# Both output gates ahead of the mLSTM, two expert buffers in the tokens' place, and ranks tile by tile in a hybrid mLSTM, HGRN2 and mixture-of-experts layer

## The chip, the cores and the metric

The kernel runs on one core of one Trainium2 chip. The metric is the device time of one execution in microseconds (us). Three runs of the kernel before took 1246.77, 1248.19 and 1250.08 us; the median is 1248.19 us.

## The reference

One layer of a diffusion backbone works on 256 latent tokens of width 1024, beside 256 context tokens that only feed the scans. All is float32.

```python
h = modulate(rms_norm(x, norm1_g), sh1, sc1)      # adaLN: six vectors from silu(c) @ w_ada
p = h @ w_in                                       # one projection, split into columns
yl_ml = sigmoid(p_o)  * head_rms(bidirectional mLSTM(q, k, v, gates), norm_g)   # 4 heads of 128
yl_hg = silu(p_go)    * head_rms(bidirectional HGRN2(q, f, i), norm_g)          # 4 heads of 128
x = x + g1 * (concat([yl_ml, yl_hg]) @ w_out)
h2 = modulate(rms_norm(x, norm2_g), sh2, sc2)
logits = h2 @ router_w + router_b                  # 32 experts
top_val, top_idx = top_k(logits, 4); gates = softmax(top_val)
# for every expert e on the tokens that chose it:
gu = xe @ w_gu[e] + b_gu[e]; glu, lin = split(gu)
y_e = (min(glu, 7) * sigmoid(1.702 * glu) * (clip(lin, -7, 7) + 1)) @ w_down[e] + b_down[e]
x = x + g2 * sum over a token's experts of gate * y_e
out = rms_norm(x, final_g)
```

## The kernel before

The latent tokens are two tiles of 128 (a = 0, 1). The kernel has two halves. The first is the mixer: norm1 and adaLN (row-vector products `gemv`, L259), the input projection, the two scans, the output projection and the router. The second is a loop over the 32 experts.

*The mixer.* The weights of a projection are split into a rounded part `wh` (ScalarE, L89) and a remainder `wl` (VectorE, L90), and the tokens into `hh` and `hl`; a product is three matmuls (L314 to L316 for products by tokens). `out_gate(c0, f0, silu)` computes one group's output gate from 1024 KB of `w_in` twice, in 96 matmuls, and stores it in `og`. Before, the HGRN2's gate (`out_gate(3600, 512, True)`) stands ahead of `rows(2, 1)`, the last `gemv`; the mLSTM's (`out_gate(1024, 0, False)`) is written behind `mlstm(0)` and `mlstm(1)`, stored by a copy (L659), and made a sigmoid in one later activation (L869). Its tokens `hh`, `hl` keep their place until then.

`mlstm(tau)` makes two passes (one for each direction) for a token tile: matmuls that spread the stabiliser `NM` (L739) and the mask (L742), exponentials on ScalarE (L751), a product with the scores on VectorE (L752), matmuls with the values `mv` (L759), and the normalisation into `ym` (L763 to L771). `through` (L782 to L784) multiplies a slice of the mixer's output by a split slice of `w_out`: 48 matmuls for the HGRN2's half, 36 split and 8 plain ones (L802) for the mLSTM's. `gated(a)` normalises `ym`, multiplies by `og` (L707), transposes (L791) and splits into `yTh`, `yTl` (L776, L777).

*From the mixer to the experts.* `project(a)` finishes the output projection of a tile and makes, in halves of 512 columns, `h2 = po * g1b` (L803), `x2 = x2 + h2` (L804), `h2 = x2 * sc2` (L805), and the sum of squares (L806). `finish(a)` transposes `h2` (L813), copies it (L814), takes the inverse root (L96 to L106), multiplies by the router's weights `rw` (L819), and picks the top four: `lg` (L820), maximum, `sel`, the tie-breaking scan (L827), `sel` again (L829), and the gates (L830 to L835). `norm2(a)` completes `h2`: tile 0 on GpSimd (L842, L843), tile 1 on VectorE (L845). Then the rank of each token within its expert: matmuls of `sel` with a triangle and with ones (L913 to L915), `posm` (L916, L918), and the counts of each expert (L920 to L924), which a conditional part behind the loop reads. Only with both tiles' ranks and `h2` can `dispatch` build the selection `S` (L945) and gather an expert's tokens by matmul (L955).

*The experts.* Expert e needs 12 MB: four loads of `w_gu` and two of `w_down`, each of 2 MB (L128). They go through buffers of 2 MB in pools that `slot()` takes in turn from the list `rings`. There are nine at the end: `ring` (3, from the start), `ring2` (3, in the mLSTM's and tokens' place on the right side, after `right_m.close()`), `ring3` (2, after `mixed.close()`) and `ring4` (1, after `front.close()`). All loads are issued in one order by the SyncE queue; a load waits for its buffer, and the ones behind it wait too. The products are L973 (`pu`), transposes L983 (`pt`), the activation, L1007 (`pd`), and the sum over experts L1019.

The order of instructions on each engine is chosen when the kernel is built: the framework's scheduler puts work in by priority and dependency, and `tc.issue_after` adds an ordering by hand. Engines then run their own list in order.

Of the kernel before, what the change touches and what calls it, by code (L numbers as in the profile page):

```python
# [28 lines left out]
def tile_hybrid_backbone(  # L29
# [26 lines left out]
    ones = fc.tile([128, 128], FT)  # L56
# [91 lines left out]
    shc = fo.tile([128, 8], FT, name="shc")  # L148
    dr = ctx.enter_context(tc.tile_pool(name="dr", bufs=1, space=bass.MemoryType.DRAM))
# [4 lines left out]
    right_m = ExitStack()  # L154
    fm = right_m.enter_context(tc.tile_pool(name="fm", bufs=1, side="right"))
    yh = fm.tile([128, 2, 512], FT, name="yh")
    mk = fm.tile([128, 2, 512], FT, name="mk")
    mq = fm.tile([128, 2, 256], FT, name="mq")
    bcol = fm.tile([128, 9, R], FT, name="bcol")
    NM = fm.tile([R, 256], FT, name="NM")  # L160
    mv = fm.tile([128, 4, 4, 130], FT, name="mv")
# [982 lines left out]
```

## Time and profile before

| | |
|---|---|
| median of three runs | 1248.19 us |
| profiled execution | 1248.19 us |
| its span (first to last instruction) | 1246.4 us |
| TensorE busy | 1136.3 us, 91% |
| VectorE busy | 423.2 us, 34% |
| ScalarE busy | 250.0 us, 20% |
| moved by the DMA queue of the weights | 452.08 MB, 87.1% of the 16 DMA engines' span |

An engine's busy share is over the whole span; stages have different limits. Time is read best in stretches: the window view gives for each stretch the busy time of every engine, the TensorE clock that was granted (1.00 is 2.4 GHz, 0.50 is 1.2 GHz), the share of DMA time in use and the rate in GB/s. The timeline gives single instructions with their start, and in brackets how long their engine had stood idle before and what released it.

### The profile page before, as it was taken

The page shows a single profiled execution, that of the slowest core. Times are in us where ns is not written, and L with a number is a line of the kernel's source. Part 1 is how long each engine was busy: PE and PEld are TensorE (multiplying, and loading weights), DVE is VectorE, ACT ScalarE, POOL GpSimd, SP SyncE. Part 2 cuts the span into 40 slices and gives each one's busy share as a digit, 9 for nine tenths or more (in the row PEclk, how much of TensorE's full clock was granted, in tenths as well). Part 3 has the DMA queues.
Part 4 walks back from the last instruction along what each step waited for, and adds up shares of the span by engine and source line. Part 5 has one row for each costly group of instructions (what it writes and reads, how often), then busy time and mean ns, then how long its engine had stood idle before and what let it go on. Part 6 is the DMA issues. An engine that isn't in the chain of part 4 may idle for free.

```text
span 1246.4 us, 14117 instructions
## 1 busy us (share of the span) xinstructions
PE 1136.3 (91%) x5790; PEld 566.7 (45%) x5791; DVE 423.2 (34%) x935; ACT 250.0 (20%) x469; POOL 102.3 (8%) x199
## 2 busy tenths in 40 slices
PE   4899999998999999989999987998899789879985
PEld 1688887886534343443334322532253234324321
DVE  5478968676112221312121211121211121112124
ACT  3577455562110000001000100100010001000001
POOL 4000002002110110120001100200020002000001
PEclk9899999997999999999999999999999999999998
DMA  9723556639799999999999999999999999999993
GB/s 372 240 73 131 202 199 235 241 124 428 326 429 426 427 427 426 415 427 427 426 427 427 428 426 429 426 427 428 427 426 426 428 428 427 427 426 427 428 427 158
DMA packets 52068, 457.30 MB, mean 367 GB/s; under 512 B 4375, under 2 KB 20848, under 8 KB 24480
## 3 DMA queue, kind: packets, MB, share of 16 engines
q1 hardware_dynamic: 50096, 452.08, 87.1%
q0 software_dynamic: 1584, 3.74, 0.9%
q8 instruction: 47, 0.77, 0.3%
q10 hardware_dynamic: 320, 0.53, 0.1%
q14 instruction: 21, 0.17, 0.0%
HBM read 455.27 MB, written 1.06 MB: 366 GB/s over the span
## 4 chain that ended last, share of the span: by engine, by line
PE 57%; DMA 37%; DVE 3%; ACT 1%; issue 1%; SPq 0%; POOL 0%; DVEq 0%; ACTq 0%
DMA w<-w_down_dram 21%; PE pu L973 19%; DMA w<-w_gu_dram 15%; PE pd L1007 7%; PE pm L955 4%; PE pm L1019 4%; PE pj L299 3%; PE pj L298 2%; PE pj L300 2%; DMA w<-w_ada_dram 2%; PE pj L259 2%; PE pt L983 1%; PE pj L316 1%; PE pj L314 1%; PE pj L315 1%; PE m L759 1%
## 5 line engine op out<-in xcount | busy, mean ns | idle before, releaser
L973 PE MATMUL pu<-w,XT 128*64 128x512 f32 x2048 | 456.4, 595 | 33.6 <-DMA w<-w_gu_dram 33.5
L973 PEld LDWEIGHTS pu<-w,XT 128*64 128x64 f32 x2048 | 142.7, 137 | 324.7 <-issue 270.3
L1007 PE MATMUL pd<-w,aT 128*64 128x512 f32 x1024 | 231.4, 597 | 17.6 <-DMA w<-w_down_dram 15.7
L1007 PEld LDWEIGHTS pd<-w,aT 128*64 128x64 f32 x1024 | 70.0, 137 | 153.8 <-issue 126.6
L990 DVE TENSOR_TENSOR gl<-pt,bgT 128x512 f32<-128x512 f32 x32 | 22.1, 692 | 335.4 <-PE pt L983 335.3
L76 ACT ACTIVATE gu<-pu 128x512 f32<-128x512 f32 x48 | 26.9, 595 | 490.9 <-PE pu L973 477.5
L78 DVE COPY gu<-pu 128x512 f32<-128x512 f32 x16 | 11.1, 692 | 244.0 <-ACT gu L76 244.0
L945 POOL TENSOR_SCALAR S<-islot,posm 128x64 f32<-128x64 f32 x60 | 25.9, 454 | 662.0 <-PE pm L955 473.1
L1010 DVE TENSOR_TENSOR YP<-pd,g2b 64x512 f32<-64x512 f32 x64 | 44.0, 688 | 93.7 <-PE pd L1007 92.9
L955 PEld LDWEIGHTS pm<-S,h 128*128 128x128 f32 x512 | 65.1, 201 | 17.4 <-issue 16.0
L955 PE MATMUL pm<-S,h 128*128 128x128 f32 x512 | 68.7, 290 | 2.2 <-DVE S L945 1.0
L1019 PE MATMUL pm<-YP,GT 128*128 128x512 f32 x128 | 61.1, 611 | 8.0 <-DVE YP L1010 8.0
L298 PE MATMUL pj<-hh,wh 128*128 128x512 f32 (+1 forms) x160 | 57.7, 368 | 3.1 <-ACT hh L361 3.1
L299 PE MATMUL pj<-hl,wh 128*128 128x512 f32 (+1 forms) x160 | 59.0, 369 | 0.1
L300 PE MATMUL pj<-hh,wl 128*128 128x512 f32 (+1 forms) x160 | 57.3, 362 | 0.0
L90 DVE TENSOR_TENSOR wl<-w,wh 128x1024 fp32r<-128x1024 f32 x39 | 47.5, 1222 | 28.0 <-ACT wh L89 27.8
L957 ACT ACTIVATE XT<-pm 128x512 f32<-128x512 f32 x32 | 19.0, 597 | 176.9 <-PE pm L955 176.9
L983 PEld LDWEIGHTS pt<-ident,gu 128*128 128x128 f32 x256 | 33.7, 210 | 35.6 <-ACT gu L76 19.7
L993 ACT ACTIVATE sg<-gl 128x512 f32<-128x512 f32 x32 | 20.2, 630 | 143.1 <-DVE gl L991 143.1
L983 PE MATMUL pt<-ident,gu 128*128 128x128 f32 x256 | 40.3, 298 | 9.1 <-ACT gu L76 9.1
L89 ACT ACTIVATE wh<-w 128x1024 fp32r<-128x1024 f32 x39 | 41.0, 1060 | 26.6 <-PE pj L299 20.1
L1019 PEld LDWEIGHTS pm<-YP,GT 128*128 128x128 f32 x128 | 22.4, 189 | 46.9 <-issue 30.0
(457 smaller groups left out, 1148.8 us busy)
## 6 DMA issues: line engine op xcount, KB each, us to landing
w<-w_gu_dram SPq DMA_DIRECT2D x128, 2048.0 KB, 34.8
w<-w_down_dram SPq DMA_DIRECT2D x63, 2048.0 KB, 35.9
w<-w_ada_dram SPq DMA_DIRECT2D x12, 2048.0 KB, 8.9
w<-w_in_dram SPq DMA_DIRECT2D x16, 1024.0 KB, 8.9
w<-w_out_dram SPq DMA_DIRECT2D x2, 2048.0 KB, 8.2
w<-w_down_dram SPq DMA_DIRECT2D x4, 512.0 KB, 30.1
xin<-x_dram SPq DMA_DIRECT2D x2, 512.0 KB, 4.1
xin<-ctx_dram SPq DMA_DIRECT2D x2, 512.0 KB, 5.7
```

What stands on the lines that cost most here:

```text
L76: act(o, i, AF.Copy)
L89: act(wh, src, AF.Copy)
L90: dve.tensor_sub(wl, src, wh.bitcast(FT))
L298: mm(o, wh[:, s], hh[:, k, t0:], start=(k == 0), stop=False)
L299: mm(o, wh[:, s], hl[:, k, t0:], start=False, stop=False)
L300: last_p[0] = mm(o, wl[:, s], hh[:, k, t0:], start=False, stop=(k == 7))
L955: mm(p_[:, i * ns:(i + 1) * ns], hv[:, a, (k + i) // 2, i % 2], S[:, a, 0:nj].rearrange("p j s -> p (j s)"), start=(a == 0), stop=(a == 1))
L973: mm(ps[64 * j:64 * j + 64, n * 512:(n + 1) * 512], XT(k), w[:, k % 2, j * 1024 + n * 512:j * 1024 + (n + 1) * 512], start=(k == 0), stop= ...
L983: nc.tensor.transpose(pt[:, f * 128:(f + 1) * 128], sv[:, f // 4, f % 4], ident)
L1007: mm(pd_[64 * n:64 * n + 64, :], aT[:, k], w[:, i, n * 512:(n + 1) * 512], start=(k == 0), stop=(k == 7))
L1010: dve.tensor_mul(yp[:, f], pd_[64 * n:64 * n + 64, :], g2b[64 * n:64 * n + 64, f])
L1019: mm(p_, GTs[j][0:ns, a * 128:(a + 1) * 128], YP[0:ns, j, n * 512:(n + 1) * 512], start=(j == 0), stop=(j == np_ - 1))
```

## The change

- The mLSTM's output gate moves up, behind `rows(2, 1)` and ahead of the mLSTM. Both gates are stored by a sigmoid directly; the copy, the later sigmoid and an exponential that only loaded a table go. The mLSTM's exponentials are ordered behind the last sigmoid.
- The tokens' place (`right`) is closed right there, and a pool `ring2` of two expert buffers opens in it. Both halves of `w_out` are loaded ahead of the mLSTM.
- The mLSTM's place becomes three fixed tiles (`place(0)` to `place(2)`), which later hold `x2`, `g2b` and `h2`. The other pools are `ring3` (1), `ring4` (2) and `ring5` (1): nine buffers as before, taken by the expert loop in a new order.
- The scale `sc2` is moved into the router's weights (`rws = rw * scc`, with `scc` from four more transposes in `rows(2, 1)`), so the router takes transposes of `x2` and not of `h2`.
- The sum of squares of a tile is added up in `project`; `h2 = x2 * sc2` comes behind it; `project(1)`'s VectorE and ScalarE work is ordered behind tile 0's sum (`late`).
- `rank(a)` makes the ranks of a tile, tile 0's from `sel` of tile 0 alone; `gates(a)` is a step of its own; `counts()` moves into the expert loop, at e = 5.

```diff
@@ out_gate @@
-            if silu:
-                act(o, ps, AF.Sigmoid)
+            last_s[0] = act(o, ps, AF.Sigmoid)
+            if silu:
                 dve.tensor_mul(o, o, ps)
-            else:
-                act(o, ps, AF.Copy)
...
@@ project, finish, rank @@
+        if late[0] is not None:
+            st_.enter_context(tc.issue_after(late[0].ins))
...
             dve.tensor_mul(h2[:, a, f], po_[a][n], g1b[:, f])
             dve.tensor_add(x2[:, a, f], x2[:, a, f], h2[:, a, f])
+            act(po_[a][n], x2[:, a, f], AF.Square, accum_out=ss[:, 2 * n + a:2 * n + a + 1])
+        late[0] = dve.tensor_add(ss[:, a:a + 1], ss[:, a:a + 1], ss[:, 2 + a:3 + a])
+        for n in range(2):
             dve.tensor_mul(h2[:, a, f], x2[:, a, f], sc2[:, f])
...
-                nc.tensor.transpose(p_[:, i * 128:(i + 1) * 128], h2[:, a, (k + i) * 128:(k + i + 1) * 128], ident)
+                nc.tensor.transpose(p_[:, i * 128:(i + 1) * 128], x2[:, a, (k + i) * 128:(k + i + 1) * 128], ident)
...
-            mm(pl[:, 0:NE], hT2[:, a, k], rw[:, k], start=(k == 0), stop=(k == 7))
+            mm(pl[:, 0:NE], hT2[:, a, k], rws[:, k], start=(k == 0), stop=(k == 7))
...
+    def rank(a, p_):
+        mm(p_[:, a * NE:(a + 1) * NE], tri, sel[:, a], start=(a == 0), stop=True, skip_group_check=True)
+        if a == 0:
+            mm(p_[:, NE:2 * NE], ones, sel[:, 0], start=False, stop=False, skip_group_check=True)
+        dve.scalar_tensor_tensor(posm[:, a], p_[:, a * NE:(a + 1) * NE], 1.0, sel[:, a], op0=OP.add, op1=OP.mult)
+        dve.tensor_scalar(posm[:, a], posm[:, a], -1.0, None, op0=OP.add)
@@ the main program @@
     out_gate(3600, 512, True)
     rows(2, 1)
+    out_gate(1024, 0, False)
+    right.close()
+    ring2 = ctx.enter_context(tc.tile_pool(name="ring2", bufs=NR2, side="right", reuse_waits="tile"))
+    wh_ = load_blocks(w_out[0], 512, 4, 0)
+    wm_ = load_blocks(w_out[0], 0, 4, 0)
...
     mlstm(0)
     mlstm(1)
-    out_gate(1024, 0, False)
...
     project(0)
     finish(0)
+    rk = bank()
+    rank(0, rk)
+    gates(0)
     project(1)
...
     finish(1)
+    rank(1, rk)
     norm2(1)
+    gates(1)
...
+    rings[:] = [(ring2, NR2), (ring, NR), (ring3, NR3), (ring4, NR4), (ring5, NR5)]
+    loaded[0] = 0
```

The built programs show what moves. Lines of the changed kernel have other numbers: L320 to L322 are the gate's matmuls, L743 and L746 the spreading of `NM` and of the mask, L764 the matmuls with the values, L787 to L789 `through`, L812 the plain half of `project`, L827 the router's transposes, L832 its product, L846 and L848 the ranks, L965 the dispatch.

TensorE from the last `gemv` into the mLSTM, before (`pj<-ident,yh` are the transposes of the HGRN2's output, L314 to L316 the mLSTM's gate):

```order
L259 MATMUL pj<-w,silr 32x512 x16
L855 MATMUL pj<-ident,yh 128x128 x4
L739 MATMUL m<-NM,ident 128x128 x3
L855 MATMUL pj<-ident,yh 128x128 x4
L739 MATMUL m<-NM,ident 128x128
L739 MATMUL t<-NM,ident 128x128 x4
L742 LDWEIGHTS idb
L742 MATMUL t<-mneg,idb 128x512
L314 MATMUL pj<-wh,hh 128x256
L315 MATMUL pj<-wl,hh 128x256
L316 MATMUL pj<-wh,hl 128x256
```

and in the changed kernel, from the end of the same gate (`fm_108` holds `yh`, `fm_109` holds `NM`):

```order
L321 MATMUL pj<-wl,hh 128x256
L322 MATMUL pj<-wh,hl 128x256
L883 MATMUL pj<-ident,fm_108 128x128 x8
L743 MATMUL m<-fm_109,ident 128x128 x4
L743 MATMUL t<-fm_109,ident 128x128 x4
L746 LDWEIGHTS idb
L746 MATMUL t<-mneg,idb 128x512
L787 MATMUL pj<-wh,yTh 128x512
L788 MATMUL pj<-wl,yTh 128x512
L787 MATMUL pj<-wh,yTh 128x512
L788 MATMUL pj<-wl,yTh 128x512
```

All 96 gate matmuls now stand ahead of the transposes and of the mLSTM, and the matmuls of `through` stand between its steps where the gate's stood.

TensorE from the end of the output projection to the dispatch, before (`h_2713` is `h2`; L906 transposes the expert biases):

```order
L906 MATMUL t<-ident,bgs 128x128 x4
L813 MATMUL m<-ident,h_2713 128x128 x8
L819 MATMUL m<-rw,hT_1927 128x32 x4
L813 MATMUL m<-ident,h_2713 128x128 x4
L819 MATMUL m<-rw,hT_1927 128x32 x4
L813 MATMUL m<-ident,h_2713 128x128 x4
L819 MATMUL m<-rw,hT_1927 128x32 x8
L913 MATMUL m<-sel,tri 128x32
L914 MATMUL m<-sel,ones 128x32
L920 MATMUL t<-sel,ones 128x32
L915 MATMUL m<-sel,tri 128x32
L921 MATMUL t<-sel,ones 128x32
```

and in the changed kernel (`fm_2347` is `x2`; the first row is the biases):

```order
L927 MATMUL t<-ident,bgs 128x128 x4
L827 MATMUL m<-ident,fm_2347 128x128 x8
L832 MATMUL m<-rws,hT_1925 128x32 x8
L846 MATMUL m<-sel,tri 128x32
L848 MATMUL m<-sel,ones 128x32
L827 MATMUL m<-ident,fm_2347 128x128 x8
L832 MATMUL m<-rws,hT_1925 128x32 x8
L846 MATMUL m<-sel,tri 128x32
L965 MATMUL pm<-S,fm_2617 128x128 x16
```

The two tiles are no longer interleaved: tile 0 is transposed and routed first, and its ranks (L846, L848), which need `sel` of tile 0, stand ahead of tile 1's transposes. The counts are gone from here.

The SyncE queue from the load of the mLSTM's gate, before (`w_3031`, `w_3041`, `w_3051`, `w_3061` are the first expert's `w_gu` in order, `w_3095` and up the loads after them; which buffer each has follows from the pools):

```order
L135 DMA w_2484<-w_in_dram 128x8x256 x2
L119 DMA w_2620<-w_out_dram 128x4x1024
L119 DMA w_2686<-w_out_dram 128x4x1024
L128 DMA w_3031<-w_gu_dram 128x4096
L128 DMA w_3061<-w_gu_dram 128x4096
L128 DMA w_3095<-w_gu_dram 128x4096
L128 DMA w_3105<-w_gu_dram 128x4096
L128 DMA w_3041<-w_gu_dram 128x4096
L128 DMA w_3136<-w_down_dram 128x4096
L128 DMA w_3051<-w_gu_dram 128x4096
L128 DMA w_3115<-w_gu_dram 128x4096
L128 DMA w_3125<-w_gu_dram 128x4096
```

and in the changed kernel (`w_3029` to `w_3059` are the first expert's `w_gu`):

```order
L136 DMA w_2152<-w_in_dram 128x8x256 x2
L120 DMA w_2275<-w_out_dram 128x4x1024
L120 DMA w_2277<-w_out_dram 128x4x1024
L129 DMA w_3049<-w_gu_dram 128x4096
L129 DMA w_3029<-w_gu_dram 128x4096
L129 DMA w_3039<-w_gu_dram 128x4096
L129 DMA w_3059<-w_gu_dram 128x4096
L129 DMA w_3103<-w_gu_dram 128x4096
L129 DMA w_3134<-w_down_dram 128x4096
L129 DMA w_3093<-w_gu_dram 128x4096
L129 DMA w_3113<-w_gu_dram 128x4096
L129 DMA w_3123<-w_gu_dram 128x4096
```

Both have `w_out` twice and then nine loads for the experts, each in the order in which the buffers come free; `w_in` and `w_out` are now issued with nothing of the mLSTM between them.

## Rows read from the trace of the kernel before

**Rows 1.** The page: the chain that ended last, by engine.

```profile
PE 57%; DMA 37%; DVE 3%; ACT 1%; issue 1%; SPq 0%; POOL 0%; DVEq 0%; ACTq 0%
```

**Rows 2.** Windows: stretch, length, busy time (instructions) of each engine, clock, DMA share, GB/s.

```profile
800.00:1200.00 400.00, 359.77 (x1668) 137.85 (x1666) 80.94 (x135) 29.42 (x53) 19.58 (x40) 1.00 1.01 427
```

**Rows 3.** Timeline of SyncE's queue: start, duration, line, transfer, count.

```profile
239.85 34.04 SPq L128 DMA_DIRECT2D w<-w_gu_dram  x5
289.89 0.33 SPq L128 DMA_DIRECT2D w<-w_down_dram  x1
291.61 5.94 SPq L128 DMA_DIRECT2D w<-w_gu_dram  x3
320.25 0.34 SPq L128 DMA_DIRECT2D w<-w_down_dram  x1
```

**Rows 4.** Timeline of TensorE, from the output projection's end to the first expert.

```profile
295.37 1.97 PE L813 MATMUL m<-ident,h 128*128 128x128 f32 x8 [3.32 <-DVE h L805]
...
302.30 3.46 PE L819 MATMUL m<-rw,hT 128*128 128x32 f32 x16
306.04 0.64 PE L913 MATMUL m<-sel,tri 128*128 128x32 f32 x2 [0.28 <-DVE sel L829]
...
310.51 5.90 PE L955 MATMUL pm<-S,h 128*128 128x128 f32 x32 [0.96 <-DVE S L945]
...
316.55 8.80 PE L973 MATMUL pu<-w,XT 128*64 128x512 f32 x40
```

**Rows 5.** Windows: the mixer's end, the stretch behind it, and two parts of that.

```profile
230.00:291.60 61.60, 61.60 (x402) 53.39 (x401) 40.54 (x126) 36.96 (x99) 2.96 (x5) 1.00 0.63 258
291.60:316.60 25.00, 19.48 (x98) 18.45 (x97) 16.72 (x70) 7.20 (x17) 8.56 (x9) 0.59 0.92 392
294.00:298.00 4.00, 2.63 (x12) 2.34 (x12) 4.00 (x18) 2.80 (x8) 0.00 (x0) 0.53 1.02 434
314.00:318.00 4.00, 4.00 (x28) 2.98 (x28) 0.00 (x0) 1.47 (x3) 1.49 (x4) 0.91 0.13 53
```

**Rows 6.** Timeline of TensorE: matmuls of the gate, then of `through`.

```profile
243.84 0.28 PE L315 MATMUL pj<-wl,hh 128*128 128x256 f32 x1
243.96 0.28 PE L316 MATMUL pj<-wh,hl 128*128 128x256 f32 x1
...
265.81 0.39 PE L784 MATMUL pj<-wh,yTl 128*128 128x512 f32 x1
266.04 0.39 PE L782 MATMUL pj<-wh,yTh 128*128 128x512 f32 x1
```

**Rows 7.** Timeline of ScalarE: an exponential of the mLSTM, a split of its output.

```profile
261.94 0.63 ACT L751 ACTIVATE E__2450<-t,bcol 128x128 f32<-128x128 f32 x2 [1.66 <-PE t L742]
...
285.56 0.37 ACT L776 ACTIVATE yTh<-t,cols 128x128 fp32r<-128x128 f32 x1 [0.42 <-DVE yTl L777]
```

**Rows 8.** Timeline of VectorE: the mLSTM, then the router.

```profile
262.60 0.43 DVE L752 TENSOR_TENSOR E__2450<-E__2450,msT 128x256 f32<-128x256 f32 x1
...
292.22 2.49 DVE L804 TENSOR_TENSOR x<-x,h 128x512 f32<-128x512 f32 x4
...
301.64 0.25 DVE L820 SCALAR_TENSOR_TENSOR lg<-m,r,rb 128x32 f32<-128x32 f32 x1 [0.80 <-PE m L819]
...
302.62 1.61 DVE L845 SCALAR_TENSOR_TENSOR h<-h,r,sh 128x512 f32<-128x512 f32 x1
304.15 1.28 DVE L827 TENSOR_TENSOR_SCAN ce<-eq 128x32 f32<-128x32 f32 x1
...
306.68 0.24 DVE L820 SCALAR_TENSOR_TENSOR lg<-m,r,rb 128x32 f32<-128x32 f32 x1
...
307.65 0.21 DVE L827 TENSOR_TENSOR_SCAN ce<-eq 128x32 f32<-128x32 f32 x1
...
308.24 0.19 DVE L829 TENSOR_TENSOR sel<-sel,eq 128x32 f32<-128x32 f32 x1
```

**Rows 9.** Timeline of GpSimd: the second half of `norm2(0)`.

```profile
302.41 2.94 POOL L843 TENSOR_TENSOR h<-h,sh 128x512 f32<-128x512 f32 x2
```

More of the change, by code (lines that the diff above doesn't have):

```diff
@@ L55, in tile_hybrid_backbone @@
     dve.tensor_scalar(ident, jp, 0.0, None, op0=OP.is_equal)
-    ones = fc.tile([128, 128], FT)
+    ones = consts.tile([128, 128], FT)
     dve.memset(ones, 1.0)
@@ L136, in load_in @@
         return v[:, 0], v[:, 1]
-    sel = fc.tile([128, 2, NE], FT, name="sel")
+    sel = keep.tile([128, 2, NE], FT, name="sel")
     pj = front.enter_context(tc.tile_pool(name="pj", bufs=4, space=PSUM))
@@ L153, in tile_hybrid_backbone, with place @@
     R = 36
[L154 to L161, printed above, removed]
+    fm = ctx.enter_context(tc.tile_pool(name="fm", bufs=1, side="right"))
+    def place(i):
+        return fm.tile([128, (2048, 1092, 2080)[i]], FT, name=f"fm{i}")
+    p0, p1, p2 = [place(i) for i in range(3)]
+    yh, mk = [p0[:, 1024 * i:1024 * i + 1024].rearrange("p (a t) -> p a t", a=2) for i in range(2)]
+    mq = p1[:, 0:512].rearrange("p (a t) -> p a t", a=2)
+    bcol = p1[:, 512:512 + 9 * R].rearrange("p (i r) -> p i r", i=9)
+    NM = p1[0:R, 836:1092]
+    mv = p2.rearrange("p (a h d) -> p a h d", a=4, h=4)
     right = ExitStack()
@@ L865, in tile_hybrid_backbone @@
     dve.tensor_add(rb, p_[:, 0:NE], rb)
-    right.close()
-    with tc.issue_after(last_e[1].ins):
-        sg_ = act(og[:, :, 0:512], og[:, :, 0:512], AF.Sigmoid)
-    with tc.issue_after(sg_.ins):
-        act(ss[:, 0:1], one_c, AF.Exp)
     po_ = [[pj.tile([128, 512], FT, name="pj") for _ in range(2)] for _ in range(2)]
-    w = load_blocks(w_out[0], 512, 4, 0)
     for k in range(4):
-        wh, wl = halves(w[:, k])
+        wh, wl = halves(wh_[:, k])
         for a in range(2):
@@ L878, in tile_hybrid_backbone @@
                 through(a, k, wh, wl, n, k == 0)
-    w = load_blocks(w_out[0], 0, 4, 0)
-    wo = [halves(w[:, 0]), halves(w[:, 1]), halves(w[:, 2]), w[:, 3]]
+    wo = [halves(wm_[:, 0]), halves(wm_[:, 1]), halves(wm_[:, 2]), wm_[:, 3]]
     fs.close()
@@ L899, in tile_hybrid_backbone @@
     finish(0)
+    rk = bank()
+    rank(0, rk)
+    gates(0)
     project(1)
     mixed.close()
-    rings.append((ctx.enter_context(tc.tile_pool(name="ring3", bufs=NR3, side="right", reuse_waits="tile")), NR3))
+    ring4 = ctx.enter_context(tc.tile_pool(name="ring4", bufs=NR4, side="right", reuse_waits="tile"))
     norm2(0)
@@ L1022, in combine, with counts @@
                 dve.tensor_add(x2[:, a, f], x2[:, a, f], p_)
+    def counts():
+        q_ = ebank()
+        mm(q_[:, 0:NE], ones, sel[:, 0], start=True, stop=False)
+        mm(q_[:, 0:NE], ones, sel[:, 1], start=False, stop=True)
+        mx = e1.tile([1, 1], FT, name="mx")
+        dve.tensor_copy(cnt_i[:, 0:NE], q_[0:1, 0:NE])
+        dve.tensor_reduce(mx, q_[0:1, 0:NE], axis=AX.X, op=OP.max)
+        dve.tensor_copy(cnt_i[:, NE:NE + 1], mx)
     def biases():
@@ L1062, in tile_hybrid_backbone @@
             next(jobs[e - 1])
+            if e == 5:
+                counts()
             if e == 7:
```

55 lines of the change are left out of this document (23 added, 32 removed).

## The prediction

> **What bounds the kernel now.** I read the chain first: 57% of the span is TensorE, 37% DMA [rows 1], so neither VectorE nor ScalarE can be worth much except where TensorE waits for them. The windows then say which stage has which limit. In the expert loop the DMA engines are full: 427 GB/s at a share of 1.01 from 800 to 1200 us [rows 2]. A load of 2 MB (2.097 million bytes) takes 2.097/0.427 = 4.91 us there. Of 192 loads for the experts nine are issued early, by 297.5 us, because there are nine buffers: 5, 1 and 3 [rows 3]. The tenth waits at 320.25 until the first expert's product, begun at 316.55 [rows 4], has freed a buffer 3.7 us later. After it 182 loads of 4.91 us, 894 us, follow nearly without a hole, and their end sets the end of the kernel. So the time follows one event, the start of the first expert's product: what moves it by 1 us moves the end by 1 us, and what moves nothing there is worth nothing.
>
> That start comes out of two stretches. In the mixer's end, 230 to 291.6 us, TensorE is busy 61.60 of 61.60 us at a granted clock of 1.00 [rows 5]: only its own work and its waits count there. From 291.6 (call this E, the end of the output projection) to 316.55, 24.95 us pass on dependencies: TensorE idles 3.32 us before the router's first transposes at 295.37, `sel` of tile 1 ends at 308.24 + 0.19 = 308.43 [rows 8], dispatch starts at 310.51 and the product 6.04 us later [rows 4]. The clock is 0.53 in the part from 294 to 298, right behind that idle time, and 0.91 only from 314 [rows 5].
>
> The sum below goes against the profiled execution, 1248.19 us with a span of 1246.4; it equals the median of the three runs.
>
> **The mixer's end: E + 1.5 us.** No matmul goes or comes in this stretch. The sigmoid stored directly takes away a copy, a sigmoid and two table loads of ScalarE. That is worth nothing: TensorE did not wait there. What does change is the cover. A pass of the mLSTM spreads `NM`, then waits for exponentials (0.63 us a pair, [rows 7]) and a product on VectorE (0.43 us, [rows 8]) before its first matmul with the values: a chain of 1.06 us, four times. Before, the gate's 96 matmuls filled these waits; they start 0.12 us apart [rows 6], 11.5 us in all. In the new order they stand in one piece ahead of the mLSTM, and the 48 matmuls of `through` fill in, 0.23 us apart [rows 6], 11.0 us. In quantity the cover is the same. But these 48 were the cover of something else: 36 of them ran while `ym` of tile 1 was normalised, transposed and split. Now `gated` has only the 36 of the mLSTM's half behind it, and the transposes of each tile stand directly ahead of the matmuls that need the split halves. A split takes 0.37 us on ScalarE after its idle 0.42 [rows 7]; I charge 0.6 us to each tile, 1.2. For the passes I charge half a chain to the first (its `through` waits for the split of the weights) and to the last, 0.4 + 0.5 = 0.9; the two between have `through` matmuls ahead in the order. Against that, the gate in one piece spares changes between kinds of work, 0.6. Sum 1.2 + 0.9 - 0.6 = +1.5. The bounds: with no wait at all and twice that sparing, -1.2; with all four chains bare (4 x 1.06 = 4.2) and 0.8 for each tile, +5.2. The four added transposes fall in `rows(2, 1)`, ahead of this stretch, at about 0.25 us each by the eight of 1.97 us [rows 4]; most of that lies beside the gate's matmuls, and it is inside these bounds.
>
> **From E to the first expert: between -0.45 and +1.0 us, taken as +0.3.** In step with the new order on TensorE:
>
> 1. Tile 0's `x2` is ready while `project(1)` still runs, since the four additions (2.49 us together, [rows 8]) no longer stand in one row behind both tiles. So the 3.32 us of idle time goes. Behind the biases the transposes of tile 0 run from about E + 0.5, and the router's product of 16 records follows. At the 0.216 us of a record in the trace (3.46/16, [rows 4]) or half of that, `lg` of tile 0 comes at about E + 5.4; before it came at 301.64, E + 10.0.
> 2. From `lg` to `sel` took 306.68 to 308.43 = 1.75 us for tile 1, with nothing between [rows 8]. For tile 0 the two halves of `norm2(1)` stand between, at least 0.75 us each (half of the 1.61 of [rows 8] rounded down): `sel` of tile 0 at E + 8.7. Before, it released the ranks at 306.04, E + 14.4 [rows 4].
> 3. Here the 5.7 us gained are given back. TensorE works in order, and the ranks of tile 0 stand ahead of tile 1's transposes, so it idles from about E + 6 until E + 8.7. Then: ranks, two pairs by 0.64 less overlap, 0.9; eight transposes, 1.9; 16 records, 3.5; `lg` to `sel`, 1.75. `sel` of tile 1 at E + 16.8. Before: 308.43 - 291.6 = E + 16.8. The interleaved order of before had tile 1's transposes and product done while VectorE still worked on tile 0.
> 4. From `sel` to the dispatch took 2.08 us, of it 0.45 for the three operations of the counts ahead of `S`; without them 1.63. Then 6.04 as before, at the same half clock. First product at E + 24.5 instead of 24.95: -0.45.
>
> The upper value is contention of VectorE and GpSimd. Beside `norm2(0)` on GpSimd (2.94 us for the second pair, 1.47 each, [rows 9]) the scan took 1.28 us, and 0.21 when GpSimd was still [rows 8]. In the new order `norm2(0)` starts at about E + 5.3 and its second pair at E + 8.4, just when `sel` of tile 0 is due. One operation put behind one half costs 1.47: -0.45 + 1.47 = +1.0. The value taken, +0.3, is the middle. As outer bounds I keep +2.1 (the scan stretched by 1.07 too) and -2.2 (tile 1's product at full clock, 3.46/2 less).
>
> The Trainium skill (SBUF — State Buffer, "Who interferes with whom") says that a VectorE instruction with two inputs in SBUF and a GpSimd instruction that reads SBUF exclude each other for a whole instruction, and that the order of issue decides who waits. The 1.28 against 0.21 us agrees. By that rule alone the wait would be full and the sum 1248.19 + 1.5 + 1.0 = 1250.7 us.
>
> **Buffers, loads, counts: 0.** Nine loads are ahead as before. Five of them go out during the mLSTM (two into the tokens' place), the other four from E on, so the DMA engines finish earlier than before and then idle some 10 us until the first buffer is freed, where they idled some 5 (53 GB/s from 314 to 318, [rows 5]). All nine are in time either way. The `gemv`'s and `w_out`'s loads stand ahead in the queue in either kernel, so nothing waits behind a new stranger. The counts' matmuls at e = 5 lie in the DMA-bound loop. If that cover were gone, they would cost about 1 us.
>
> Sum: 1248.19 + 1.5 + 0.3 = **1250.0 us**. A measurement of this kernel can tell about 0.3%, 3.7 us, from no change: 1244.4 to 1251.9.
>
> **Rivals.**
>
> *The cover was needed (slower).* If the matmuls of `through` can't start when the passes need them, since their split weights come from the same ScalarE and VectorE that make the exponentials, every pass shows its chain and each tile its split: E + 5.2, and with +0.3 the time is 1253.7 us. It decides from E + 3.4 on, two bare chains more than I charge. For it: ScalarE is busy 36.96 and VectorE 40.54 of the 61.6 us [rows 5], so they are no idle helpers. Against: 11.0 us of cover for 4.2 us of chains.
>
> *The clock holds (faster).* TensorE is fed from E on without the 3.32 us of idle time. If it stays at 1.00, the dispatch takes half of its 5.90 us, tile 1's product half of 3.46 and its transposes half of 1.97: 5.7 us less. 1248.19 + 1.5 - 0.45 - 5.7 = 1243.5 us. Against: step 3 leaves TensorE idle at E + 6 for some 2.7 us, and the trace's clock was down right behind 3.3 idle us; it came back only in the dense work of the dispatch and the product. The Trainium skill (TensorE: Matmul & The Clock Gate, Part 1) says that the clock follows how busy the engine has been of late; the rows agree, and this rival turns on whether the new idle time is as harmful as the old.
>
> *Earlier loads shorten the stream (faster).* If the DMA hole before 320.25 (from about 315, 5.3 us) closed, the time would be 1242.9. Against: the cap is nine buffers, and the tenth load needs the first product.
>
> *The ranks are not tile by tile in effect.* Step 3 is already this case: tile 0's ranks wait at the head of TensorE's queue. If `sel` of tile 0 is late by both stretches, this is the +2.1 above, 1251.8.
>
> **How the numbers follow.** Forecast 0.52, its own range 1247 to 1252.3; uncovered mLSTM 0.29; clock 0.13; earlier loads 0.04; the remaining 0.02 lies beyond. Faster by over 0.3% comes from the two faster rivals, 0.17. Slower by over 0.3% comes from the 0.29 and a sliver of the forecast, 0.31. Between: 0.52. The range goes from 1243.5 to 1255.0: it takes in the clock's case and the slower rival with 1.3 us on top, and leaves out little more than the earlier loads.
>
> **What would show it.** The last plain matmul of `project` at 293 (right) or beyond 295 (uncovered). TensorE's idle time ahead of the first rank near 2.7 us, released by VectorE's `sel`; `sel` of tile 0 at E + 8.7 and of tile 1 at E + 16.8. The granted clock in the dispatch near 0.5; near 1.00 it would be the clock rival. The tenth load 3.7 us behind the first product, and the rate in the loop at 427 GB/s: another rate would make the whole account wrong.

## The result and the profile after

The changed kernel takes 1255.4 us (median of four runs, 1254.52 to 1256.58) where the kernel before takes 1249.13 beside it: ratio 1.0054 [1.0042, 1.0066], slower by 6.3 us. The forecast was 1250.0 us with a range of 1243.5 to 1255.0. The profiled execution took 1254.78 us, its span is 1252.9.

First the chain by engine on the page, the answer to [rows 1]:

```profile
PE 56%; DMA 35%; issue 3%; DVE 3%; ACT 1%; POOL 0%; SPq 0%; DVEq 0%; ACTq 0%; POOLq 0%
```

TensorE and DMA give up three points, and "issue" gains two. Where the time lies shows in the windows (columns as in [rows 5]): the mixer's end, the stretch from there to the first expert's product, three pieces of the first pass of the mLSTM, and the loop.

```profile
229.25:295.88 66.63, 64.89 (x406) 55.77 (x407) 43.14 (x133) 33.35 (x98) 2.97 (x5) 0.97 0.67 263
295.88:323.85 27.97, 16.12 (x93) 15.10 (x92) 16.55 (x68) 6.41 (x15) 8.37 (x9) 0.63 0.69 293
249.00:251.00 2.00, 2.00 (x13) 1.88 (x13) 1.78 (x5) 2.00 (x10) 0.00 (x0) 0.78 0.94 395
251.00:253.00 2.00, 2.00 (x10) 1.85 (x9) 0.82 (x5) 1.45 (x7) 0.00 (x0) 0.50 1.08 455
253.00:255.00 2.00, 2.00 (x13) 1.78 (x12) 1.12 (x7) 0.75 (x3) 0.00 (x0) 0.87 0.98 412
800.00:1200.00 400.00, 360.74 (x1684) 138.64 (x1683) 79.01 (x132) 30.30 (x55) 23.52 (x48) 1.00 1.01 427
```

The loop stands as in [rows 2], 427 GB/s at a share of 1.01. The mixer's end, counted from the last `gemv` to the last matmul of `project`, is 66.63 us long at a granted clock of 0.97 with 1.74 us in which TensorE is idle; before it was 61.76 us (229.82 to 291.58) and busy throughout. It begins 0.57 us earlier, so E moves from 291.58 to 295.88: **+4.30**. The stretch behind E is 27.97 us instead of 24.97: **+3.00**. Together +7.30 at the first product.

SyncE's queue, against [rows 3], shows that this goes on to the end:

```profile
234.70 48.08 SPq L129 DMA_DIRECT2D w<-w_gu_dram  x5
294.24 0.33 SPq L129 DMA_DIRECT2D w<-w_down_dram  x1
295.91 5.18 SPq L129 DMA_DIRECT2D w<-w_gu_dram  x3
327.54 0.33 SPq L129 DMA_DIRECT2D w<-w_down_dram  x1
```

The tenth load is issued at 327.54, 3.69 us behind the product at 323.85, and 7.29 us later than before. The last group of `pd` products begins 6.60 us later (1228.68 against 1222.08), the span is 6.5 us longer: the loop gives back 0.8 at most. Nine loads are still early, and the stretch behind E shows a DMA share of 0.69 where [rows 5] had 0.92: idle DMA time that costs nothing, since the tenth load waits for the first product either way.

The waits of TensorE in the mixer's end (who waits, for whom, sum, count, longest); before, this list is empty:

```profile
PE pj L787 <- ACT yTh L781: 0.9, 2, 0.5
PE t L796 <- DVE rb L897: 0.3, 1, 0.3
PE m L764 <- DVE E__2571 L757: 0.2, 1, 0.2
PE m L764 <- DVE E__2360 L757: 0.2, 1, 0.2
```

The tail on TensorE, against [rows 4]:

```profile
296.19 1.04 PE L827 MATMUL m<-ident,fm 128*128 128x128 f32 x8
297.98 1.97 PE L832 MATMUL m<-rws,hT 128*128 128x32 f32 x16 [0.75 <-ACT hT L828]
308.49 0.61 PE L846 MATMUL m<-sel,tri 128*128 128x32 f32 x2 [8.54 <-DVE sel L842]
...
309.34 1.95 PE L827 MATMUL m<-ident,fm 128*128 128x128 f32 x8
311.18 3.62 PE L832 MATMUL m<-rws,hT 128*128 128x32 f32 x16
316.66 0.64 PE L846 MATMUL m<-sel,tri 128*128 128x32 f32 x2 [1.86 <-DVE sel L842]
318.00 5.70 PE L965 MATMUL pm<-S,fm 128*128 128x128 f32 x32 [0.70 <-DVE posm L850]
...
323.85 6.66 PE L983 MATMUL pu<-w,XT 128*64 128x512 f32 x30
```

TensorE idles 8.54 us before tile 0's first rank. On VectorE, against [rows 8]:

```profile
293.19 1.29 DVE L813 TENSOR_TENSOR fm<-pj,row 128x512 f32<-128x512 f32 x2 [1.58 <-DMA row<-scr]
...
302.27 0.25 DVE L833 SCALAR_TENSOR_TENSOR lg<-m,r,rb 128x32 f32<-128x32 f32 x1
...
304.57 1.38 DVE L868 SCALAR_TENSOR_TENSOR fm<-fm,r,sh 128x512 f32<-128x512 f32 x2
...
306.05 1.07 DVE L841 SCALAR_TENSOR_TENSOR eq<-ce,cg,eq 128x32 f32<-128x32 f32 x1
307.16 1.19 DVE L842 TENSOR_TENSOR sel<-sel,eq 128x32 f32<-128x32 f32 x1
...
316.13 0.25 DVE L841 SCALAR_TENSOR_TENSOR eq<-ce,cg,eq 128x32 f32<-128x32 f32 x1
316.42 0.19 DVE L842 TENSOR_TENSOR sel<-sel,eq 128x32 f32<-128x32 f32 x1
```

and GpSimd, against [rows 9]:

```profile
302.33 3.12 POOL L865 TENSOR_SCALAR fm<-fm,r 128x512 f32<-128x512 f32 x2 [18.91 <-DVE rt L103]
305.42 2.87 POOL L866 TENSOR_TENSOR fm<-fm,sh 128x512 f32<-128x512 f32 x2
```

VectorE works without a wait of note from 293.19 to 309.1. TensorE has tile 0's product at 299.95 (297.98 + 1.97), E + 4.1, but `lg` comes at 302.27, E + 6.4, behind VectorE's other work; from there to `sel` (308.35) 6.1 us pass, since two halves of `norm2(1)` stand between (1.38 us) and most small operations beside GpSimd's 5.99 us are longer than for tile 1, when GpSimd is still: the pair ahead of `sel` takes 1.07 and 1.19 us against 0.25 and 0.19. Then the same clock as before: tile 1's product takes 3.62 us, the dispatch 5.70.

### The profile page after: what moved, and what is told of

It reads as the page before. It is cut to its first block, busy times and chain, and to the rows that moved or that the text cites. A ratio compares the mean times of both kernels' runs of the same rounds, so it can differ in the third digit from the quotient of the medians.

```text
span 1252.9 us, 14137 instructions
## 1 busy us (share of the span) xinstructions
PE 1138.8 (91%) x5794; PEld 567.0 (45%) x5795; DVE 425.6 (34%) x939; ACT 245.6 (20%) x465; POOL 102.0 (8%) x199
## 4 chain that ended last, share of the span: by engine, by line
PE 56%; DMA 35%; issue 3%; DVE 3%; ACT 1%; POOL 0%; SPq 0%; DVEq 0%; ACTq 0%; POOLq 0%
PE pu L983 19%; DMA w<-w_down_dram 18%; DMA w<-w_gu_dram 15%; PE pd L1017 10%; PE pm L965 5%; PE pm L1029 3%; PE pj L305 3%; PE pj L306 2%; PE pj L304 2%; PE pj L265 2%; PE pt L993 2%; PE pj L322 1%; PE pj L320 1%; PE pj L321 1%; PE m L547 1%
## 5 line engine op out<-in xcount | busy, mean ns | idle before, releaser
L1020 DVE TENSOR_TENSOR YP<-pd,fm 64x512 f32<-64x512 f32 x64 | 44.0, 688 | 132.6 <-PE pd L1017 131.8
L965 PEld LDWEIGHTS pm<-S,fm 128*128 128x128 f32 x512 | 66.2, 205 | 17.7 <-issue 16.3
L965 PE MATMUL pm<-S,fm 128*128 128x128 f32 x512 | 70.5, 294 | 1.9 <-POOL S L955 0.9
```

Source lines behind the costliest of these rows:

```text
L965: mm(p_[:, i * ns:(i + 1) * ns], hv[:, a, (k + i) // 2, i % 2], S[:, a, 0:nj].rearrange("p j s -> p (j s)"), start=(a == 0), stop=(a == 1))
L1020: dve.tensor_mul(yp[:, f], pd_[64 * n:64 * n + 64, :], g2b[64 * n:64 * n + 64, f])
```

## The experiments

Each was timed beside the kernel before, whose median was 1248.73 to 1249.03 us there; ratios are against it. "E" and "product" are from each one's profiled execution; "mixer" runs from the last `gemv` to E, "stretch" from E to the first expert's product.

| kernel | mixer, clock | E | stretch | product | median us | ratio |
|---|---|---|---|---|---|---|
| before | 61.76, 1.00 | 291.58 | 24.97 | 316.55 | 1249.13 | |
| after | 66.63, 0.97 | 295.88 | 27.97 | 323.85 | 1255.4 | 1.0054 [1.0042, 1.0066] |
| gate only | 66.15, 0.97 | 295.81 | 24.22 | 320.03 | 1251.55 | 1.0019 [1.0010, 1.0029] |
| gate half | 67.26, 0.97 | 297.13 | 24.26 | 321.39 | 1255.1 | 1.0055 [1.0038, 1.0071] |
| gate double | 74.38, 1.00 | 304.19 | 24.20 | 328.39 | 1260.62 | 1.0101 [1.0083, 1.0118] |
| router part only | 69.08, 0.95 | 297.32 | 30.48 | 327.80 | 1259.46 | 1.0089 [1.0072, 1.0106] |
| router part, mixer kept | 63.78, 1.00 | 293.31 | 31.31 | 324.62 | 1257.56 | 1.0071 [1.0054, 1.0088] |
| ranks late | 64.97, 1.00 | 295.96 | 22.71 | 318.67 | 1249.55 | 1.0008 [0.9999, 1.0018] |
| no GpSimd | 66.59, 0.97 | 295.80 | 26.82 | 322.62 | 1254.19 | 1.0044 [1.0030, 1.0058] |
| ranks late, no GpSimd | 68.21, 0.95 | 296.67 | 18.92 | 315.59 | 1247.05 | 0.9984 [0.9973, 0.9996] |
| ranks late, rows first | 68.18, 0.95 | 297.80 | 21.38 | 319.18 | 1248.91 | 0.9997 [0.9987, 1.0007] |
| the last two together | 66.64, 0.97 | 296.24 | 18.12 | 314.36 | 1245.6 | 0.9974 [0.9964, 0.9983] |
| mixer of before, new router | 63.78, 1.00 | 293.13 | 20.51 | 313.64 | 1245.69 | 0.9973 [0.9964, 0.9983] |

**The mixer: gate only.** The kernel before, with the mLSTM's gate ahead of the mLSTM, its sigmoid stored directly and the exponentials ordered behind it; router and buffers as before.

```diff
     rows(2, 1)
+    out_gate(1024, 0, False)
...
     mlstm(1)
-    out_gate(1024, 0, False)
```

> The kernel before with one part of the change: the mLSTM's output gate ahead of the mLSTM, stored by a sigmoid directly. Pools, loads, router and ranks stay as before. Theory A (the mixer's end got longer because the gate no longer fills the mLSTM's waits): the output projection ends 3 to 5 us later than in the kernel before, the stretch from there to the first expert stays at 25.0 us, and the time is 1252 to 1254 us. Rival B (the mixer's end got longer through the new places, the buffers or the transposes in the last rows, and the gate is innocent): the output projection ends within 1 us of before, 1249 us.

E comes at 295.81 against 295.88 of the whole change, the mixer takes 66.15 us, and the waits are the same four. So nearly all of the change's loss in the mixer comes with the gate's move alone (4.39 of 4.87 us), as A has it. The profiled product is 3.5 us later than before; by the ratio the time is up 2.4 us [1.2, 3.6], and the median lies 0.45 below A's range: the stretch behind E came out at 24.22 and not 25.0.

**Gate double.** The gate computed twice: ahead of the mLSTM, and again where it was. That adds 96 matmuls and restores the filler.

```diff
     rows(2, 1)
+    out_gate(1024, 0, False)
```

> The kernel before with the mLSTM's gate computed twice: 96 matmuls added ahead of the mLSTM (their result is overwritten), and the gate behind it in the code as before, so that its 96 matmuls still stand between the mLSTM's steps. The 96 added cost 96 x 0.12 = 11.5 us of TensorE's time if nothing else changes. Theory A (what the moved gate costs is the cover it takes from the mLSTM): with the cover back the output projection ends 11 to 12.5 us later than in the kernel before, at 302.5 to 304, and the time is 1260 to 1262 us; so the 96 matmuls between the steps cost only some 7 us of end time, since the kernel with the gate in front alone ended at 295.8. Rival B (a gate in front delays the mixer by itself, through its weights' loads or the exponentials that start later): it ends at 306 to 308, 15 us or more later, time 1264 to 1266.

The window of its mixer's end:

```profile
229.80:304.19 74.39, 74.31 (x500) 65.21 (x499) 46.57 (x133) 41.44 (x105) 2.96 (x5) 1.00 0.62 241
```

TensorE is busy for 74.31 of 74.39 us at 1.00. Against before, 96 matmuls ahead cost 74.38 - 61.76 = 12.6 us; against gate only, the same 96 as filler cost 74.38 - 66.15 = 8.2 us. The difference, 4.4 us, is by arithmetic the same as gate only less before (66.15 - 61.76); what this run adds is that a gate ahead, with the old filler kept, has neither the waits nor the drop of the clock. So both go with the filler's absence and not with the gate's early place. The time is A's, and E is 0.2 us beyond A's range. This kernel has 96 matmuls more than gate only, though: whether the amount of filler decides, or what the filler waits for, it does not tell.

**Gate half.** 48 of the 96 matmuls ahead, 48 behind.

```diff
+    out_gate(1024, 0, False, (0,))
...
-    out_gate(1024, 0, False)
+    out_gate(1024, 0, False, (1,))
```

> The kernel before with one half of the mLSTM's gate (48 of 96 matmuls) ahead of the mLSTM and the other half behind it in the code as before; storing by a copy and the later sigmoid as before. Theory A (what the gate costs in front is the cover that the mLSTM's waits lose): with half of the cover left the output projection ends at 291.5 to 293 us, TensorE idles under 1 us in the mixer's end, and the time is 1248.5 to 1250 us. Rival B (any matmuls of through inside the mLSTM cost the clock and the time): it ends at 294 to 296, time 1251 to 1252.5.

It came out later than gate only by 1.3 us at E, beyond A and B, with a wait that was not foreseen:

```profile
PE t L795 <- DVE rb L870: 2.8, 1, 2.8
```

Here the late sigmoid is kept, and ScalarE's two table loads and the activation (272.99 to 276.7) stand ahead of the splits of `w_out`; VectorE's remainders `wl` wait for these, and `rb` stands behind them. This kernel says nothing of the filler's size.

**The router part only.** The kernel before with the new `project`, `finish`, `rank`, `gates` and `counts` and the four added transposes, but its own gate and buffers.

```diff
     project(0)
     finish(0)
+    rk = bank()
+    rank(0, rk)
+    gates(0)
     project(1)
...
     finish(1)
+    rank(1, rk)
     norm2(1)
+    gates(1)
```

> The kernel before with the other part of the change: router on transposes of x2, sums and ranks tile by tile, counts in the expert loop; the gate stays behind the mLSTM, pools and loads as before. Theory A (tile 0's ranks at the head of TensorE's queue give back what tile 0 gains; the rows' late arrival and GpSimd make it worse only where the mLSTM ends late): the output projection ends within 0.5 us of before, the stretch from there to the first expert takes 22 to 25 us, time 1246 to 1249 us. Rival B (the new order of the router is itself the loss, whatever the mixer does): the stretch takes 27 to 28 us as in the changed kernel, time 1251.5 to 1253.

Neither theory held, because the mixer did not stay as it was: TensorE's order there changed with the four transposes in `rows(2, 1)`, and the mixer took 69.08 us with these waits, which are not those of the changed kernel:

```profile
PE pj L785 <- DVE yTl L778: 2.6, 1, 2.6
...
PE pj L783 <- ACT yTh L777: 1.0, 1, 1.0
```

So the transposes were put behind the mLSTM:

```diff
-            o, j = (shc, 2) if gp == 1 else (scc, 0)
-            dve.tensor_copy(o.rearrange(...), columns(bank(True), t)[:, j:j + 2, :, 0])
...
+    dve.tensor_copy(scc.rearrange(...), columns(bank(True), ars[2])[:, 0:2, :, 0])
     dve.tensor_tensor(rws, rw, ...)
```

> The router's part of the change once more on the kernel before, with its four added transposes behind the mLSTM and not in the last rows, so that the mixer's matmuls stand in nearly the order of before. Theory A (the late end of the mixer in the first run of this part came from a reshuffled order of the mixer, not from the router): the output projection ends within 1.5 us of before (291.6), the stretch behind it takes 27 to 30 us as TensorE waits for tile 0's selection, time 1252 to 1255 us. Rival B (the ordering of project(1) behind tile 0's sum holds up the mixer itself): the output projection ends at 295 to 297 us and the time is 1257 to 1260.

The mixer is at 63.78 us, 2.0 us longer than before with one wait of 1.0 for `yTh`, and the clock at 1.00. E is 1.7 us later than before and so just outside A's 1.5; the stretch is 31.31, 6.3 us longer than before and beyond A, with two long waits:

```profile
296.65 2.01 PE L828 MATMUL m<-rws,hT 128*128 128x32 f32 x16 [2.00 <-ACT hT L824]
309.44 0.60 PE L842 MATMUL m<-sel,tri 128*128 128x32 f32 x2 [10.78 <-DVE sel L838]
```

10.78 us before the first rank, and 2.0 for a copy on ScalarE behind the copy of the biases. The router part by itself is a loss, product +8.07. With gate only's +3.48 that makes 11.55, not 7.30: the parts can't be added.

Most of the difference is an order on ScalarE that the changed kernel does not have. Here the copy of the biases, which needs transposes that TensorE makes behind `project`, stands ahead of tile 0's squares; tile 0's sum needs the squares, and tile 1's additions are ordered behind that sum:

```profile
293.82 1.09 ACT L931 ACTIVATE bgT<-t 128x512 f32<-128x512 f32 x1 [5.38 <-PE t L930]
294.70 0.70 ACT L811 ACTIVATE pj<-x 128x512 f32<-128x512 f32 x1
...
296.15 0.16 DVE L812 TENSOR_TENSOR ss<-ss 128x1 f32<-128x1 f32 x1 [5.72 <-ACT pj L811]
```

VectorE idles 5.72 us, and `lg` of tile 0 comes at 302.94, E + 9.6. In the changed kernel the squares (295.11) stand ahead of the copy (296.39), `lg` comes at E + 6.4, and the stretch is 3.3 us shorter.

**Ranks late.** The changed kernel with tile 0's ranks behind tile 1's router.

```diff
     finish(0)
-    rk = bank()
-    rank(0, rk)
...
     finish(1)
+    rk = bank()
+    rank(0, rk)
     rank(1, rk)
```

> The changed kernel with the ranks of tile 0 put behind the router of tile 1, so that tile 1's transposes and product on TensorE wait for nothing of tile 0's selection. Theory A (the 8.5 us that TensorE idled ahead of tile 0's ranks delayed tile 1 by nearly as much): the stretch from the output projection to the first expert falls from 28.0 to 20 to 22 us, time 1248 to 1250 us. Rival B (VectorE's queue holds tile 1 anyway: its inverse root, its two halves of norm2 and tile 0's selection stand ahead of tile 1's, beside GpSimd): it falls by 2 us or less, time 1253.5 to 1255.

E is where it was (295.96), by chance: the mixer began 1.74 us later and, without the drop of the clock, took 1.66 less. The stretch is 5.26 us shorter, 0.7 above A's range; the time falls by 5.9 (1255.4 to 1249.55), to A's. Tile 1's transposes and product now run in the idle time:

```profile
299.86 1.69 PE L827 MATMUL m<-ident,fm 128*128 128x128 f32 x8
301.45 3.62 PE L832 MATMUL m<-rws,hT 128*128 128x32 f32 x16
309.46 0.61 PE L846 MATMUL m<-sel,tri 128*128 128x32 f32 x2 [4.38 <-DVE cg L837]
```

4.38 us of idle time are left, and VectorE's rows beside GpSimd show why:

```profile
306.01 1.69 DVE L868 SCALAR_TENSOR_TENSOR fm<-fm,r,sh 128x512 f32<-128x512 f32 x1
307.72 1.14 DVE L841 SCALAR_TENSOR_TENSOR eq<-ce,cg,eq 128x32 f32<-128x32 f32 x1
```

**No GpSimd.** `norm2(0)` on VectorE as `norm2(1)` is, once with the ranks as changed and once with the ranks late.

```diff
-            if a == 0:
-                nc.gpsimd.tensor_scalar(h2[:, a, f], ...)
-                nc.gpsimd.tensor_add(h2[:, a, f], ...)
-            else:
+            if True:
                 dve.scalar_tensor_tensor(h2[:, a, f], ...)
```

> The changed kernel with norm2 of tile 0 on VectorE like that of tile 1; GpSimd does nothing there. Theory A (the selection of tile 0 took 6.1 us from its logits, where tile 1's took 1.8, because VectorE's small operations stood beside GpSimd's): the selection of tile 0 takes about 4.6 us (1.8 and four halves of 0.7), the first expert starts 1 to 2 us earlier, time 1253.5 to 1254.5 us. Rival B (the two halves on VectorE cost what the contention cost): 1255 us, no change.

> The changed kernel with tile 0's ranks behind tile 1's router and norm2 of tile 0 on VectorE; the rows are fetched as in the change. The kernel with the three edits started its first expert at 314.4, that with the late ranks alone at 318.7. Theory A (GpSimd beside VectorE costs more than the rows' arrival: in the late-rank kernel VectorE's small operations took 0.4 to 1.7 us instead of 0.2 to 0.7): first expert at 315.5 to 316.5, time 1246.5 to 1247.5. Rival B (the rows' arrival is the larger part): 317 to 318, time 1248 to 1249.

With the ranks as changed, the pair ahead of `sel` is short again and `sel` of tile 0 comes at 306.22 instead of 308.35:

```profile
305.75 0.25 DVE L841 SCALAR_TENSOR_TENSOR eq<-ce,cg,eq 128x32 f32<-128x32 f32 x1
306.03 0.19 DVE L842 TENSOR_TENSOR sel<-sel,eq 128x32 f32<-128x32 f32 x1
```

but VectorE now does GpSimd's work too, and the stretch gains only 1.15 us (27.97 to 26.82). With the ranks late it gains 22.71 - 18.92 = 3.8 us. In both runs the numbers are A's, but with the ranks as changed the interval of the ratio overlaps that of the changed kernel, so the gain in time is not clear of noise there. What GpSimd's contention is worth depends on who waits for VectorE.

**Rows first.** The chain of the changed kernel (start, length, what) holds one DMA of 10.80 us: the row `g1b`, which GpSimd issues at 282.36 behind the row `g2b`. Ahead of these stand 38.21 us of "issue", in which GpSimd's queue waited for a place; they are the points that "issue" gained.

```profile
243.59 38.21 issue
...
282.36 10.80 DMA row<-scr
```

In this kernel, which has the ranks late too, `g2b` goes last.

```diff
-    nc.gpsimd.dma_start(sc2, bcast(scr[1, 0:D], D))
-    nc.gpsimd.dma_start(g2b, bcast(scr[1, D:2 * D], D))
+    sc2_d = nc.gpsimd.dma_start(sc2, bcast(scr[1, 0:D], D))
+    with tc.issue_after(sc2_d.ins):
+        nc.gpsimd.dma_start(g2b, bcast(scr[1, D:2 * D], D))
```

> The changed kernel with tile 0's ranks behind tile 1's router and the rows g1b and sc2 ahead of g2b on GpSimd's queue; norm2 of tile 0 stays on GpSimd. Theory A (the rows are worth the 1.6 us that VectorE waited for them, no more): first expert at 316.5 to 317.5, time 1247.5 to 1248.5. Rival B (with the rows early the whole chain of tile 0 moves before the end of the output projection, and it is worth 3 us or more): 315 to 316, time 1246 to 1247.

> The changed kernel with three edits: ranks of tile 0 behind the router of tile 1, the rows g1b and sc2 fetched ahead of g2b on GpSimd's queue, norm2 of tile 0 on VectorE. With the first alone the first expert started at 318.7. Theory A (of the rest, the contention with GpSimd and the rows' arrival are worth 1 to 2.5 us together): first expert at 316 to 317.5, time 1247 to 1248.5. Rival B (VectorE's total of work binds there, and the two halves of norm2 eat what is gained): 318 to 319, time 1249 to 1250.

The stretch is 1.3 us shorter (22.71 to 21.38; without GpSimd 0.8, 18.92 to 18.12), but in the first of the two the mixer ran at a clock of 0.95 instead of 1.00 and E came 1.84 us later, so the first product (319.18) moved the wrong way; that of the second (314.36) came earlier than either theory had it. Both expectations missed. In time neither can be told from its twin without the rows. With `norm2(0)` on VectorE as well the kernel takes 1245.6 us and beats before and after.

**The mixer of before with a mended router.** Router part with the mixer kept, ranks late, no GpSimd, the biases moved down (`sq` holds the last square of `project`):

```diff
     finish(0)
-    rk = bank()
-    rank(0, rk)
...
     finish(1)
+    rk = bank()
+    rank(0, rk)
     rank(1, rk)
...
     gates(1)
+    p_ = bank(True)
+    for i in range(4):
+        nc.tensor.transpose(p_[:, i * 128:(i + 1) * 128], bgs[:, i::4], ident)
+    with tc.issue_after(sq[0].ins):
+        act(bgT.rearrange(...), p_.rearrange(...), AF.Copy)
```

> The mixer of the kernel before (gate behind the mLSTM, four added transposes behind it too) with the router of the change (transposes of x2, sums tile by tile, counts in the loop), but ranks of both tiles behind both routers, norm2 of both tiles on VectorE, and the expert biases' copy on ScalarE behind the squares. Theory A (the router's part gains once nothing stands at the head of TensorE's queue and the mixer is not lengthened): output projection within 1 us of 291.6, first expert at 309 to 313 us instead of 316.55, time 1242 to 1246 us. Rival B (VectorE's chain for tile 1 is as long as before whatever tile 0 gains): first expert at 315 to 317, 1247 to 1249.

1245.69 us, as fast as the kernel above, and the time that A gave; E is 1.5 us later than before, where A allowed 1, and the first product 0.6 later than A's range. With the biases' copy behind the squares `lg` of tile 0 comes at 299.85, E + 6.7, where it was E + 9.6. Its E is 3.1 us earlier (293.13 against 296.24), its stretch 2.4 us longer; TensorE still idles 4.67 us ahead of the first rank:

```profile
304.62 0.60 PE L843 MATMUL m<-sel,tri 128*128 128x32 f32 x2 [4.67 <-DVE top L832]
```

## Why the prediction was wrong

Its frame held: one event, the first product, sets the end (+7.30 there, +6.5 in the span), no cost of buffers and loads shows, and the clock was low for most of the stretch behind E (0.63 over it), so the clock rival fell. Two terms failed, both too small, and each for something that I had put at nothing: the clock inside the mixer, and VectorE's queue and most of GpSimd's contention ahead of tile 0's `sel`.

**"The mixer's end: E + 1.5 us" measured +4.3.** That is within its bounds, and beyond the E + 3.4 from which I let the rival "the cover was needed" decide (two chains more than the 1.5 would be 3.6; it is beyond that too). But the waits were not what I had too small: TensorE idles 1.74 us, 0.9 of it for `yTh`, 0.4 for VectorE's products with the scores and 0.3 for the router's bias `rb`, where I had charged 1.2 + 0.9 = 2.1, and the rival's four bare chains (4.2 us) did not come. What I had put at nothing is the clock inside the mixer; I had looked for a change of it behind E only. By the windows above it was 0.78, 0.50 and 0.87 for three pieces of 2 us, and 2 x (0.22 + 0.50 + 0.13) = 1.7 us. Ranks late has the same order in the mixer and the same four waits without the drop, and its mixer is 1.66 us shorter. Of the +4.87 of the mixer's length the waits and the clock make 3.4; the other 1.4 are busy time. Gate only, which has no transposes added, has the same waits and a drop of the same size and is 0.5 us shorter; the last 1.0 I did not separate, and the 0.6 that I took off for fewer changes between kinds of work shows in no run.

Gate double shows that waits and drop go with the filler that was moved away. That they go because `through` depends on ScalarE and VectorE, and the gate's 96 matmuls on nothing that the mLSTM makes, is argued: with the gate ahead there are also 96 matmuls fewer to fill with, and no run keeps the amount and changes the kind.

**Step 2, "`sel` of tile 0 at E + 8.7", measured E + 12.5; so TensorE idled 8.5 us where step 3 had 2.7.** The mechanism of step 3 was right: tile 0's ranks stand at the head of TensorE's queue, and ranks late shows that they cost 5.3 us. The size went wrong twice ahead of it. First, `lg` came at E + 6.4, not E + 5.4, and VectorE held it, not the product on TensorE that I had reckoned with (done at E + 4.1): VectorE started the additions 1.58 us late, waiting for the DMA of the row `g1b`, which stands on GpSimd's queue behind `g2b`, whose place the mLSTM held until its end (the rows were issued at 281.81 to 283.4 instead of 269.2 to 270.8), and tile 1's additions (L813 at 296.87 and on) and two inverse roots stand ahead of `lg`. Second, from `lg` to `sel` 6.1 us passed, not 3.3: I had charged contention to one operation (1.47 us) and it falls on most of them. The terms from `sel` to `sel` (8.26 against 8.1) and from `sel` to the product (7.24 against 7.67) were close. 1.0 + 2.8 + 0.2 - 0.4 = 3.5 on top of the -0.45 that steps 1 to 4 gave: the +3.0 measured.

The Trainium skill (SBUF — State Buffer, "Who interferes with whom") has VectorE's operations with two inputs in SBUF excluded by a GpSimd operation that reads SBUF. The trace agrees: 1.07 and 1.19 us beside GpSimd, 0.25 and 0.19 in the kernel without it. I named that rule and applied it to one operation in place of all that stand between `lg` and `sel`. Comparisons of one tile with a column were longer beside GpSimd too (`eq` 0.60 us against 0.25 for tile 1); whether they were held up themselves or stood in line behind another, the trace does not show.

The outer bound of +2.1 for the stretch was passed, and the rival of late ranks (1251.8 us) was priced too low, mainly for one reason: I took the 1.75 us from `lg` to `sel` from tile 1, where GpSimd and VectorE's queue are free, and used it for tile 0, where neither is. With GpSimd's work and the ranks' place at the head of TensorE's queue both taken away (ranks late, no GpSimd) the stretch is 18.92 us, 9 us below the changed kernel's.

What stays open: the 1.0 us of the mixer; whether the amount of filler or its kind decides there; and why the clock drops in some executions and not in others. Why the two parts cost 4.25 us less together than apart is open in part: the biases' copy on ScalarE makes some 3 us of it (`lg` 3.2 us later), the rest I did not separate.

## What to carry to other kernels

Before moving work ahead, ask what is left to fill the waits behind it, how much of it, and whom it waits for itself; look at the clock of the stretch that it left, and not only at its idle time. An instruction that depends on another engine belongs behind the independent work of its in-order queue, however early its own inputs seem; and when a small chain on VectorE decides, add GpSimd's contention to every operation in it, and look at whose work it stands behind. An entry of 10.8 us in the chain is not worth 10.8 us (here 0.8 to 1.3 of the stretch): ask what is late next. And a part of a change that is tried alone can be put into another order on every engine: look at its trace before its time is called the part's price.

## What was not expected of the hardware

The same order of TensorE's instructions in the mixer took 64.97, 66.6 and 68.2 us in six profiled executions, at a mean clock of 1.00, 0.97 and 0.95. The difference is one stretch at 1.2 GHz in the first pass. The windows of ranks late, and of ranks late without GpSimd:

```profile
249.00:251.00 2.00, 2.00 (x14) 1.76 (x15) 1.82 (x5) 2.00 (x9) 0.00 (x0) 1.00 1.01 422
251.00:253.00 2.00, 2.00 (x17) 1.84 (x16) 1.52 (x5) 2.00 (x10) 0.00 (x0) 1.00 1.00 422
253.00:255.00 2.00, 2.00 (x14) 1.82 (x13) 1.86 (x9) 1.81 (x8) 0.00 (x0) 1.00 1.02 426
```

```profile
249.00:251.00 2.00, 2.00 (x10) 1.77 (x9) 0.99 (x3) 1.75 (x7) 0.00 (x0) 0.50 1.02 430
251.00:253.00 2.00, 2.00 (x11) 1.85 (x10) 0.84 (x5) 1.04 (x4) 0.00 (x0) 0.50 1.01 420
253.00:255.00 2.00, 2.00 (x9) 1.81 (x9) 0.81 (x6) 0.73 (x3) 0.00 (x0) 0.50 1.00 422
```

The changed kernel's three rows, further up, lie between these two. Such a drop came in five of the six, and in gate only. Around its start, from 245 to 249 us, TensorE was busy for 3.69 to 3.71 of 4.00 us in all seven; in before, in gate double and in the two kernels with before's mixer at 1.00 it was busy for 4.00, and the clock did not drop. The rows of before and of the changed kernel:

```profile
245.00:249.00 4.00, 4.00 (x38) 4.00 (x36) 1.95 (x5) 1.54 (x2) 0.00 (x0) 1.00 0.66 279
245.00:249.00 4.00, 3.69 (x22) 2.54 (x20) 2.88 (x8) 3.99 (x16) 0.00 (x0) 1.00 1.00 414
```

So small holes went with the risk, not with the certainty, of a drop; that they cause it is not shown, since the matmuls of this stretch differ as well. Each size of the drop cost 1.6 us more.

The Trainium skill (TensorE: Matmul & The Clock Gate, Part 1) says that the clock follows how busy TensorE has been of late, and, of its rise at the start of sustained work, that the point varies from run to run; these rows, of kernels with one order in the mixer, agree with the first and show the like for a fall. The E of one profiled execution thus carries some 1.6 us either way, so the experiments on the router are read by their stretches, and the times by all executions.
